# A two-layer GLA and differential-attention trunk: first root from token-major x, turned attention weights in pieces of 512 bytes, another stored order

## The chip, the cores and the metric

The kernel runs on one core of a Trainium2 chip. The metric is the device time of one execution in microseconds (us). A core has engines that run side by side: TensorE (PE; its weight loads are listed apart as PEld), VectorE (DVE), ScalarE (ACT), GpSimd (POOL), and SyncE (SP), which in this kernel issues every transfer (DMA). Each engine works through its own queue in order, so an instruction that waits holds up all that stand behind it.

## The reference, cut to what matters

x is 2048 tokens by 1024 features, in float32. Two layers; each computes

```python
h = rms_norm(x, norm_g[l]) * (1.0 + scale[:, None]) + shift[:, None]   # scale, shift from c
proj = h @ w_in[l]                                     # 1024 -> 3600 columns, split in nine
gqkv = silu(causal_depthwise_conv(gq, gk, gv))         # 4 taps
o_gla  = gla_branch(...)    # 4 heads: per chunk of 64 tokens state = a * state + k_dec^T v, o = q state
# diff_branch, 4 heads with two 64-wide maps each, block-causal in chunks of 64:
s = einsum('bqhmd,bkhmd->bhmqk', qi, k);  p = softmax(where(mask, s, -inf))
attn = p[:, :, 0] - lam * p[:, :, 1]
o = einsum('bhqk,bkhe->bqhe', attn, v)                 # then rms_norm, gate
x = x + gate[:, None] * (concat([o_gla, o_diff]) @ w_out[l])
```

`rms_norm` needs, for each token, the root of the mean of its 1024 squares. The last product of the attention, o = attn v (PV), sums over keys. TensorE sums over the partitions of its stationary operand, so the weights must lie with the keys on the partitions, while the softmax leaves them with the queries there: each 128x128 tile of weights has to be turned.

## The kernel before, in words

**Tiling.** The 2048 tokens are four units u of 512 (UT); a unit is four tiles of 128 (TT, P). Activations are feature-major (features on partitions, eight blocks k of 128; KT). The projections and the output projection work in split precision: a float32 operand is split in a rounded high part and a low rest (`hi`, `lo`), and three matmuls of 128x128 by 512 columns replace one. The score matmuls use two, the PV matmuls plain float32; TensorE shows each PV matmul as two records.

**Streams.** Python generators write the work of one kind each: `dense_stream` (projections of 9 weight items and the output), `gla_stream`, `qk_stream`, `attn_stream`, `prep_stream` (the normalized h of the next unit), `ada_stream` (modulation). `run_streams` interleaves them by a rough clock: `yield pe(cost, wait)` lets time pass, `yield need(event, lag)` holds a generator until another calls `done(event)`. Nothing is issued yet: `Program.record` notes each operation with what it depends on.

**Order.** `Program.order` is a list scheduler. It prices each operation (`cost`), gives tile buffers in the order in which they were recorded, adds prices such as a change of matmul `mode`, and picks on each engine, among what is ready, the operation with the smallest turn. The turns are the recorded order plus a stored list of steps, `ORDER` (a compressed text at the end of the file), which `found_order` unpacks. The engines get their instructions in the resulting order, for good: line 351 of the profile is where all of them are issued, so instructions are told apart by tiles.

**Start** (`start`, line 658). The vectors, c, and the first unit's x (feature-major, four transfers of 512 KB to tiles `xp`) are loaded. The squares of the eight feature blocks are made on ACT and summed on DVE into `sqs` (`add_square`); `sum_squares` sums over partitions with float32 matmuls against ones; `root` scales on DVE (`xms`) and takes the power on GpSimd (`rs`); four scaled identities and matmuls with ones spread the root to all partitions (`rsb`). Then, for each k, two DVE passes over a modulation weight tile `wm` give scale and shift, `make_h` makes `hhi` and `hlo`, and 24 matmuls of the first two projection items (0 and 4) follow, with weights `raw` split on ACT and DVE to `w`.

**Preparation of the later units** (`prep_gen`, line 634). In layer 0 a unit's x is loaded token-major (`xt`, four transfers of 512 KB), ACT squares it with an accumulated sum per token (`xss`), `rs_write` makes the root, transposes it and writes it to DRAM (`rd`); it is read back spread over partitions (`rsb`). This begins when the h of the unit before is done, plus 6 us of the rough clock. `make_h` waits for the event `free_h`. Tiles `xt`, `xp`, `la`, `E`, `qh`, `ql` share four buffers.

**GLA** (`gla_gen`, line 785). The gates pass through `la`, cumulative sums by matmuls with `trir`, and `E`, their exponential on ACT; transposes of the convolved keys and values (`uT`) follow, the values' ending with the event `vtr`; then the scan with 64x64 float32 matmuls (`Sn`, `vN`).

**Attention** (`attn_gen`, line 1005). For each head and query tile qt both score maps are made, reduced to a minimum by DVE, exponentiated on ACT into tiles `s` of up to 2048 keys, and combined on DVE into `at`. The weights of the unit's own keys are transposed on TensorE (`flip`). Those of earlier units' keys are *turned* (`turn_blocks`, line 1061) in units 1 and 2, and in unit 3 for heads 0 to 2: DVE transposes 32x32 blocks into `b`, a transfer writes `b` to a DRAM buffer `ad`, another reads it back to `at` with the blocks exchanged between partition groups. Two key blocks are interleaved element by element, so the read moves runs of 2 x 32 = 64 words (256 bytes), and `pv` (line 1072) loads each key block as stationary operand with a step of two words. V is stored in a matching order of rows (`vp`).

Of the kernel before, what the change touches and what calls it, by code (L numbers as in the profile page):

```python
# [13 lines left out]
F32 = mybir.dt.float32  # L14
# [110 lines left out]
class Program:  # L125
# [54 lines left out]
    def cost(e, method, args, kw, out):  # L180
        n = math.prod(out.shape[1:])
        if e == "S":
            return math.prod(out.shape) * 4 / {64: 208.0, 256: 326.0}.get(out.shape[-1], 350.0)
# [23 lines left out]
    def mode(op):  # L207
# [4 lines left out]
        return 1 if (k, m) == (CH, CH) else 2 if m == 32 else 0  # L212

# [13 lines left out]
    def order(self, turn_of):  # L227
# [27 lines left out]
        res, burst, mode = [], 0, 0  # L255
        while len(res) < N:
# [98 lines left out]
def trunk_kernel(ctx, tc, xl, x, c, ccol, w_ada, w_mod, w_all, w_glr, w_gk, vecs, lam, out):  # L355
# [278 lines left out]
    def prep_gen(l, u, xsrc):  # L634
        key = l * NU + u
        if l == 0:
            yield need("h", key - 1, lag=6.0)
            ss = p_sm.tile([P, TT], F32, tag="xss", name="xss", bufs=2)
            for t in range(TT):
# [3 lines left out]
                yield pe(0, 2.0)  # L643
            rs_write(key, ss)
# [13 lines left out]
    def start():  # L658
# [6 lines left out]
        sqs = p_x.tile([P, UT], F32, tag="sqs", name="sqs")  # L665
# [6 lines left out]
        for c_ in range(KT // 2):  # L672
# [9 lines left out]
        V.tensor_scalar(cact, cact, 0.5, None, op0=ALU.mult)  # L682
        wm = [mod_load(0)]
# [17 lines left out]
        for k in range(KT):  # L701
            if k % 2 and k + 1 < KT:
                for it in FIRST:
# [234 lines left out]
    AD = [[dram.tile([2 * u, P, 4, 64], F32, name=f"ad{u}_{t}") for t in range(2 * TT)] if u else None  # L938
# [66 lines left out]
    def attn_gen(l, u, hd):  # L1005
# [55 lines left out]
        def turn_blocks(at, b, dr):  # L1061

            n = u * UT
            src = at[:, 0:n].rearrange("p (g k a i) -> p g k a i", k=2, a=4, i=32)
            dst = b[:, 0:n].rearrange("p (g a i k) -> p g k a i", a=4, k=2, i=32)
            for k in range(2):
                V.transpose(dst[:, :, k], src[:, :, k])
            SY.dma_start(dr.rearrange("g p b n -> p g (b n)"), b[:, 0:n].rearrange("p (g n) -> p g n", n=256))
            SY.dma_start(at[:, 0:n].rearrange("p (h n) -> p h n", n=64),
                         dr.rearrange("g (a j) b n -> (j b) (g a) n", a=4))  # L1070

        def pv(qt):
# [19 lines left out]
            if turned:  # L1092
                pairs = at[:, 0:u * UT].rearrange("p (g m k) -> p g k m", k=2, m=P)
# [4 lines left out]
                for j in range(u):  # L1098
                    mmv(4 * j, 4, lambda k: pairs[:, k // 2, k % 2, :], False, j == u - 1)
# [218 lines left out]
def _layouts(x, c, w_ada, b_ada, norm_g, w_in, conv_w, w_gk, b_gk, gla_norm_g, qn_g, kn_g, lam_q1, lam_k1, lam_q2,  # L1318
# [25 lines left out]
    '{Wp48S^xk9=GL@E0stWa8~^|S5YJf5;FqgLq+I|2U>bnck+!@@V3AjytBp45^Tr3;$E~Z9ORR0R@5I(P6(V1^7&ZjV2!e;h2L-hkd023f?~QmHvy'  # L1344
    'fVakgbngi`>5pSg!9l?VM7NkTVkBM~8!=J<NRDIXxkw7gR>+Mzu#6ox-7gALO}P(vg^BQ|*#<DX6#e_Ss5mBRgq7-fGY*lsojHoNzyEiIa4UJWz8'
    'c#AtO|+deNLnfv>aknmGZ#JNvnX-Uu_G1P2cy%qJ4uh9B~8%EzPjvuT+HL=dBv@@?D3fG(Nrf>XNCz=^(mtyf7LUVR%@S#A9a+WvCZ(Toy!b+jDJ'
    'id$_S$)6>jQ$z@m)6UfabaK`+Oi>BaMz^;fF%?VT(0DlHe9sqDm_55`_o)!lXg*2Z`^vB0sZ!$Z2mAw*$z8sRQhT-<u~{nb%%n(I9{=A?7IQXo`}'
    'oX%VtS2;IPT<_e79BjY^~Fe*l9P(-HoSN~M23h|0<p!3`aHg#=PAe@IYNree>oF0Fc)zH|6K7~!>KWGLxeIviTYeaiyZ7@*HeIXf&AME8t5wxXiP'
    '0T{Ig0K@0N*k$uhgE88;;ZL;F(h%{_l3{1lM5MGgGxf@yRhGQs*mKFG8%KERO}?x02?Z9%`#AeB{IFM}p0pnTQa$TQR>9udIO;=-_5{Lt(4C!R+@'
    'ByJ#10S4YQwmkvbRkDf}YOq0(*mMPK^%(28Y0@7^Y-`<J{JDv*a)-N8FmaQ%ndNT(4YPH6#lSokDgAjKzr53NKjLJN>k^o&c-zdWCb`05~oX`uwh'  # L1350
    '|8A%aNL?0^YrziZ7C4uXwt8H1-FWuX$!ruQ6OvwxbA}q)lJ*_Lt4lR#P+JU913#>`6;lYN9EgX`Bnh8kLmL#mfd;naoRP0JV<5GF2-yPgwpOf>H6'
    'r9%$6pRjJ_nUv_BRl#|V~VO7Tg>QVb<#u5eex<ea+vla2edqnbd03__qM`GZ2gPm6_yh~U)P)1l@ppX?dqs8Zy8`QH0h>}D4CG5`ClE=z|9~_cIy'
    'BnRV%P`M!F)|`h^<I6$mPt{WvoGwyNb0@>090HwJGKf{U`J)YbJk!`Ls6qz~3#^W8fr+-kM+Q70Wlv!MpTY9fS3d8c51b}40IutrQpYN{(d19R%l'
    '0j2WIIs64$!pK-L>h5j=jXpmQCygS><q}PTHfy_jwi+6mEIxxZj)kNx{7-uE*5Q<lOsWeH(S7{j_b{b~qVEkl#G`u$3;~Vy1qsN~H)6TuRW5eif*'
    'SX%a}fh4>xwDJt1{cTQqu$snK-r#c2*R6J~Xr2xgEem!eS8t)M0EjFUgNcR*C~MOnmuhs$!;Fldg78;Q1cc0~<KazD}<^g5yK&tVlEck3Xvp-aIU'
    '0O@n8`3GbyzQSdDV{4_CH4*reN;eB>aY4o;nZ<D(!v4N)iktF13C~q3Y_7v>M2_&Q8Uo>>HZy-KCVsMSG*UgDwk&UU1S5(|ppP0C?Cw(|Ae1G*Mr'
    '0tQJbhqq{n<-VocAx3=!CI<qk=HCN%K!{}Aq)3R_z06^H}>)i`bM%hC3h}wljZshV%g2vX}Q%&`BaX^CqPK6UHZ~vxD|w{?2NYt_arRB5W%Z9Tq)'
    'r+bTe0rLFQNEr?IdGA7wm;6${Ajg1UX-{7$9Sy5)`Bsp?gND*5hWx9PXyKh8ypIJQ!AJe-KdeTuE~FNQTB!TdlIjY4X*J;DXB#3nL8g_F}r8L5g0'
    'laaoRJJarB$7Dj%I1xO02E>2a+M}WzCjK#8>yTqm1q0jHEF|DJq_wVAH&?8A+L;@pfT5jt!b2#hN}aK0$=}{vWWXDozC+*u2wP!An7idnS{sy0pC'
    '7lJHbscX$?M{YKzUF^I%9^T4=H|^g!sP;bI2_-B&mYl=Se`2sm?wef{Gu&)&^`@^%lrThhCixq+43I8ES3zOT~KF9UurJzjOWwGDR0+k4zZ)CVjk'  # L1360
# [208 lines left out]
```

## Time and profile before

| | |
|---|---|
| median of 3 runs | 2433.13 us (2430.43 to 2433.43) |
| the profiled execution | 2430.82 us, span 2428.7 us |
| TensorE with work in flight | 2372.0 us (98% of the span) |
| VectorE / ScalarE / GpSimd busy | 1829.6 / 1230.7 / 125.6 us |
| transfers | 573.77 MB, 369,525 packets, mean 236 GB/s |

The span runs from the first to the last instruction on the core. A matmul's busy time is modelled, and matmuls overlap: the distance from start to start of two neighbours tells what one takes. A group's row reads: line, engine, operation, out<-in by the program's names, shape, count | busy us, mean ns of one | idle time of the engine just before them, and what ended it. In the order of time a row gives its start, its length, and in brackets how long the engine stood idle before it and for what.

### The profile page before, as it was taken

The page shows a single profiled execution, that of the slowest core. Times are in us where ns is not written, and L with a number is a line of the kernel's source. Part 1 is how long each engine was busy: PE and PEld are TensorE (multiplying, and loading weights), DVE is VectorE, ACT ScalarE, POOL GpSimd, SP SyncE. Part 2 cuts the span into 40 slices and gives each one's busy share as a digit, 9 for nine tenths or more (in the row PEclk, how much of TensorE's full clock was granted, in tenths as well). Part 3 has the DMA queues.
Part 4 walks back from the last instruction along what each step waited for, and adds up shares of the span by engine and source line. Part 5 has one row for each costly group of instructions (what it writes and reads, how often), then busy time and mean ns, then how long its engine had stood idle before and what let it go on. Part 6 is the DMA issues. An engine that isn't in the chain of part 4 may idle for free.

```text
span 2428.7 us, 38475 instructions
## 1 busy us (share of the span) xinstructions
PE 2372.0 (98%) x12903; PEld 1945.9 (80%) x12903; DVE 1829.6 (75%) x5166; ACT 1230.7 (51%) x2726; POOL 125.6 (5%) x400
## 2 busy tenths in 40 slices
PE   6899999999999999999999999999999999999999
PEld 5687787888888888888788787888788887888887
DVE  8868886897568967589865894668746798747894
ACT  3766653556335553355663574346524556324552
POOL 0000000000000000000000000000000000000000
PEclk9899999999999999999999999999999999999999
DMA  7657997787776778587557777666667867775764
GB/s 293 241 193 259 324 338 245 251 270 239 246 230 204 248 223 276 171 247 236 181 198 270 270 276 263 215 222 216 211 244 231 244 205 235 232 257 172 232 193 150
DMA packets 369525, 573.77 MB, mean 236 GB/s; under 512 B 191824, under 2 KB 251696, under 8 KB 366256
## 3 DMA queue, kind: packets, MB, share of 16 engines
q1 hardware_dynamic: 369328, 571.32, 71.6%
q8 instruction: 102, 1.67, 0.3%
q14 instruction: 95, 0.78, 0.1%
HBM read 416.03 MB, written 161.50 MB: 238 GB/s over the span
## 4 chain that ended last, share of the span: by engine, by line
PE 78%; DVE 11%; ACT 4%; DMA 4%; issue 2%; POOL 0%; SPq 0%; DVEq 0%; ACTq 0%; POOLq 0%
PE acc L351 52%; PE sc L351 12%; PE po L351 9%; PE tp L351 5%; DVE s L351 4%; DMA w<-wd 2%; ACT s L351 1%; DVE w L351 1%; DVE t L351 1%; DVE xp L351 1%; ACT la L351 1%; DMA xp<-xd 1%; DVE vN L351 1%; DVE hlo L351 1%; DMA wr<-in_w_ada_dram 1%
## 5 line engine op out<-in xcount | busy, mean ns | idle before, releaser
L351 PE MATMUL acc<-w,hhi 128*128 128x512 f32 x2560 | 844.8, 405 | 7.0 <-DVE t L351 2.9
L351 PEld LDWEIGHTS acc<-w,hhi 128*128 128x128 f32 x2560 | 467.1, 189 | 102.3 <-DVE t L351 4.1
L351 PE MATMUL acc<-w,hlo 128*128 128x512 f32 x1280 | 496.5, 402 | 0.3 <-DVE hlo L351 0.3
L351 ACT ACTIVATE s<-s,mx 128x1280 f32<-128x1280 f32 (+15 forms) x256 | 308.3, 1205 | 317.0 <-DVE s L351 201.5
L351 DVE TENSOR_SCALAR_CACHE_REDUCE s<-sc,mx 64x64 f32<-64x64 f32 (+5 forms) x640 | 307.1, 483 | 61.8 <-PE sc L351 44.1
L351 PE MATMUL acc<-oh,w 128*128 128x512 f32 x1024 | 335.9, 398 | 2.0 <-DMA w<-wd 1.6
L351 PE MATMUL acc<-hhi,w 128*128 128x512 f32 x960 | 323.3, 401 | 0.6 <-DVE z L351 0.4
L351 PEld LDWEIGHTS acc<-w,hlo 128*128 128x128 f32 x1280 | 240.6, 189 | 45.8 <-issue 0.9
L351 PEld LDWEIGHTS po<-Vj,s 128*128 128x128 f32 x1536 | 215.6, 196 | 13.7 <-issue 0.6
L351 PEld LDWEIGHTS acc<-oh,w 128*128 128x128 f32 x1024 | 190.5, 188 | 44.2 <-DMA w<-wd 2.7
L351 PE MATMUL po<-Vj,s 128*128 128x128 f32 x1536 | 221.8, 280 | 0.0
L351 DVE TENSOR_SCALAR_CACHE_REDUCE s<-sc 128x512 f32<-128x512 f32 (+4 forms) x256 | 157.9, 620 | 80.9 <-PE sc L351 44.7
L351 PEld LDWEIGHTS acc<-hhi,w 128*128 128x128 f32 x960 | 178.0, 188 | 37.3 <-DVE z L351 1.1
L351 DVE SCALAR_TENSOR_TENSOR s<-s,r 128x512 f32<-128x512 f32 (+3 forms) x320 | 201.2, 666 | 3.6
L351 PE MATMUL acc<-ol,w 128*128 128x512 f32 x512 | 199.7, 397 | 0.0
L351 PE MATMUL acc<-hlo,w 128*128 128x512 f32 x480 | 189.3, 399 | 0.0
L351 PE MATMUL sc<-Kj,qh 128*128 128x512 f32 x384 | 157.6, 416 | 1.6 <-DVE s L351 0.9
L351 PE MATMUL sc<-Kj,ql 128*128 128x512 f32 x384 | 150.7, 398 | 0.0
L351 POOL MEMSET s<- 64x64 f32 x256 | 37.3, 146 | 2084.6 <-PE po L351 1150.7
L351 DVE SCALAR_TENSOR_TENSOR t<-ub,vec,t 128x512 f32<-128x512 f32 x192 | 138.8, 745 | 7.1 <-ACT t L351 6.4
L351 ACT CAST w<-raw 128x512 fp32r<-128x512 f32 x160 | 97.2, 622 | 79.0 <-PE acc L351 58.2
L351 DVE TENSOR_TENSOR w<-raw,w 128x512 fp32r<-128x512 f32 x160 | 108.1, 685 | 33.5 <-ACT w L351 32.8
(185 smaller groups left out, 3643.5 us busy)
## 6 DMA issues: line engine op xcount, KB each, us to landing
w<-wd SPq DMA_DIRECT2D x416, 512.0 KB, 4.5
wd<-w SPq DMA_DIRECT2D x144, 512.0 KB, 5.1
raw<-in_w_all_dram SPq DMA_DIRECT2D x80, 512.0 KB, 4.7
Kj<-kd SPq DMA_DIRECT2D x48, 512.0 KB, 6.1
ad<-s SPq DMA_DIRECT2D x24, 768.0 KB, 5.2
s<-ad SPq DMA_DIRECT2D x24, 768.0 KB, 6.9
wr<-in_w_ada_dram SPq DMA_DIRECT2D x128, 128.0 KB, 3.7
ad<-s SPq DMA_DIRECT2D x32, 512.0 KB, 4.0
```

The source lines that it names most:

```text
L351: getattr(self.engines[e], method)(*[real(a) for a in args], **{k: real(v) for k, v in kw.items()})
```

## The change

1. *Start.* The root of the first unit comes from token-major x, as in the later units: four transfers of 512 KB to tiles `xt` (in the ring of `s`), four Squares on ACT with accumulated sums, and `root` of these. The feature-major x, still wanted by `make_h`, is loaded one pair of blocks at a time, the first before the first modulation weights, the others in the loop over k. The eight squares, seven adds and the sums by matmul go.
2. *Preparation.* In layer 0 it begins at the event `vtr` of the unit before in place of `h` plus 6, and the rough clock lets 8 us pass between the squares and the root.
3. *Turned weights.* Four key blocks are interleaved instead of two: four DVE transposes per tile, each a quarter of the row, writing with a step of four words; `ad` is half as many groups with 128-word rows; the transfer out has runs of 512 words, the one back runs of 128 words (512 bytes); `pv` loads the stationary operand with a step of four words.
4. *Planner and order.* The price of a transfer by run length gets an entry for 128; a 64x64 matmul is priced at 70 ns instead of 54; a change to a `short` operation (a transpose, or a plain float32 matmul) costs 32 ns. `ORDER` is another stored list.

```diff
-                return 54 if args[1].shape[0] == CH else 60
+                return 70 if args[1].shape[0] == CH else 60
...
+                if self.short(ops[i]) != brief:
+                    brief = not brief
+                    t += 32 if brief else 0
...
-            yield need("h", key - 1, lag=6.0)
+            yield need("vtr", key - 1)
...
                 yield pe(0, 2.0)
+            yield pe(0, 8.0)
             rs_write(key, ss)
...
-        sqs = p_x.tile([P, UT], F32, tag="sqs", name="sqs")
+        ss = p_sm.tile([P, TT], F32, tag="xss", name="xss", bufs=2)
+        xt = []
+        for t in range(TT):
+            if t % 2 == 0:
+                xt.append(p_s.tile([P, 2, D], F32, tag="s", name="xt"))
+            SY.dma_start(xt[-1][:, t % 2, :], x[t * P:t * P + P, :])
...
+        x_load(0)
         wm = [mod_load(0)]
...
-        for k in range(KT):
-            add_square(sqs, xs[k // 2][:, k % 2, :], k == 0)
-        root(sum_squares(sqs))
+        for t in range(TT):
+            A.activation(xt[t // 2][:, t % 2, :], xt[t // 2][:, t % 2, :], AF.Square, accum_out=ss[:, t:t + 1])
+        root(ss)
...
             if k % 2 and k + 1 < KT:
+                x_load((k + 1) // 2)
...
-    AD = [[dram.tile([2 * u, P, 4, 64], F32, name=f"ad{u}_{t}") for t in range(2 * TT)] if u else None
+    AD = [[dram.tile([u, P, 4, 128], F32, name=f"ad{u}_{t}") for t in range(2 * TT)] if u else None
...
-            src = at[:, 0:n].rearrange("p (g k a i) -> p g k a i", k=2, a=4, i=32)
-            dst = b[:, 0:n].rearrange("p (g a i k) -> p g k a i", a=4, k=2, i=32)
-            for k in range(2):
+            src = at[:, 0:n].rearrange("p (g k a i) -> p g k a i", k=4, a=4, i=32)
+            dst = b[:, 0:n].rearrange("p (g a i k) -> p g k a i", a=4, k=4, i=32)
+            for k in range(4):
                 V.transpose(dst[:, :, k], src[:, :, k])
-            SY.dma_start(dr.rearrange("g p b n -> p g (b n)"), b[:, 0:n].rearrange("p (g n) -> p g n", n=256))
-            SY.dma_start(at[:, 0:n].rearrange("p (h n) -> p h n", n=64),
+            SY.dma_start(dr.rearrange("g p b n -> p g (b n)"), b[:, 0:n].rearrange("p (g n) -> p g n", n=UT))
+            SY.dma_start(at[:, 0:n].rearrange("p (h n) -> p h n", n=P),
                          dr.rearrange("g (a j) b n -> (j b) (g a) n", a=4))
...
-                pairs = at[:, 0:u * UT].rearrange("p (g m k) -> p g k m", k=2, m=P)
+                pairs = at[:, 0:u * UT].rearrange("p (g m k) -> p g k m", k=4, m=P)
...
-                    mmv(4 * j, 4, lambda k: pairs[:, k // 2, k % 2, :], False, j == u - 1)
+                    mmv(4 * j, 4, lambda k: pairs[:, k // 4, k % 4, :], False, j == u - 1)
```

More of the change, by code (lines that the diff above doesn't have):

```diff
@@ L182, in cost @@
         if e == "S":
-            return math.prod(out.shape) * 4 / {64: 208.0, 256: 326.0}.get(out.shape[-1], 350.0)
+            return math.prod(out.shape) * 4 / {64: 208.0, 128: 277.0, 256: 326.0}.get(out.shape[-1], 350.0)
         if e == "T":
@@ L212, in mode, with short @@
         return 1 if (k, m) == (CH, CH) else 2 if m == 32 else 0
+    @staticmethod
+    def short(op):
+        return op[1] == "transpose" or op[2][2].dt == F32
     @staticmethod
@@ L254, in order @@
         work, win = {}, 3413
-        res, burst, mode = [], 0, 0
+        res, burst, mode, brief = [], 0, 0, True
         while len(res) < N:
@@ L670, in mod_load, with x_load @@
             return wm
-        for c_ in range(KT // 2):
+        def x_load(c_):
             xp = p_q.tile([P, 2, UT], F32, tag="q", name="xp")
@@ L1343 @@
 ORDER = (
[L1344 to L1358, printed above, removed]
@@ new lines @@
+    'OnuYWqg5GaamQH5fW#>e-^KB9gyIphC-t+Aigfi?VUBm|IFVMf|GX2hqjNL;y+Yyw8*gF3V813_Jm7(I>vQ4OTyl@!Qjnk_>@IqP9b>Xz<M0wIMk'
+    'FL502k##i1FSE*mOcHOLd9hey2Cl~z%D~L=CTuJOXm~OdpOCx@b{gkcFd^(!V{NZ-Cob3Lm|;AB;TrKXAX3JmKAtDIQS6>@icA#33D!<iJbl?g=J'
+    'O>?NHhRY;1on5%Kpi?74zu8-4isa+5n@to*$*<dF9q1mlI}eBN|Pc9-E7zP|qDB*v#PnIu4*y?e-BdEckOc3PFC@4xJ*gqi|YCVEP1fKOHP>e<pn'
+    'Kta!|Oq;EhBriDZ)EpO+faaAmuja@?hQ@$o6R*AzqGy>?;?`HX+6L0b_j#@0!#QO*e1DZ&FWn`V4B<p_-6!`D&JlYm|MK^1=R~YXQTHN+$i#bAmF'
+    'YkQ90=z}YQ&;=^ZEcR63?xj2mcDH1L2pWy{xZy?xijg;;Lj(jBh2=obf2DVKrwPlXrMAKg5^6pFjArg6~Wxu~2Ccppi+P3QSecP}~4`X-N_rG2ek'
@@ L1547 @@
+    'l{DK(D<hT2NJ03vMk<AroSsH>%^|p5`mOPF7EY~%E(6CUCXYJHy945pa6(!Q+ALB+UCc$y3@`M7A9t)c*5fWyzz{p!}8B1RBtQy&80I8GZ<~QO{i'
+    'b2X&#3NWrj~k4iNwBv0Q~*%(u|xT+>}Q@q2UJLuyqqqgg18j>1aw%q?!=r|7koawyOha+qDudf)*s$hG=zsHVb)fduVA=!lt*(Quz9?&^MS*W>rv'
+    'jTQQf&$j7Kr07?$#yjJEItP};2WWF`{HkV$U%gx#1x8suQ~DjFu0zW_lw+ViSf&pI}u$_cIj%qnfpS+12#ZMAk@n)rQ5q5uE@b$-I?hP&IR00FOv'
+    '0rs&1XBw=qvBYQl0ssI200dcD'
 )
```

375 lines of the change are left out of this document (187 added, 188 removed).

## The prediction

> **What bounds the kernel now.** I read the page first: busy times, then the chain of work that ended last.
>
> ```profile
> span 2428.7 us, 38475 instructions
> PE 2372.0 (98%) x12903; PEld 1945.9 (80%) x12903; DVE 1829.6 (75%) x5166; ACT 1230.7 (51%) x2726; POOL 125.6 (5%) x400
> ...
> PE 78%; DVE 11%; ACT 4%; DMA 4%; issue 2%; POOL 0%; SPq 0%; DVEq 0%; ACTq 0%; POOLq 0%
> ```
>
> TensorE has work in flight for 2372.0 of 2428.7 us. So only two things move the time: what its own instructions take, and the 56.7 us in which it stands idle. The profiled execution took 2430.8 us, 2.1 us more than its span; the median of the three runs shown is 2433.1, another 2.3 us (0.1%) above. I sum against 2430.8.
>
> Next, the view of who waited for whom, for TensorE alone, and the table of busy times by stretches of 50 us (columns: PE, PEld, DVE, ACT, POOL, granted clock, DMA share, GB/s).
>
> ```profile
> PE sc L351 <- DVE sqs L351: 17.0, 1, 17.0
> PE tp L351 <- ACT E L351: 9.7, 2, 9.3
> PE tp L351 <- DVE s L351: 4.7, 6, 2.1
> PE acc L351 <- DMA w<-wd: 2.3, 6, 0.7
> ...
> 0.00:50.00 50.00, 27.63 (x109) 22.98 (x110) 39.29 (x104) 18.18 (x29) 2.40 (x11) 1.00 0.88 340
> 100.00:150.00 50.00, 38.06 (x179) 30.82 (x179) 31.99 (x118) 29.24 (x91) 4.55 (x15) 0.83 0.50 176
> ...
> 1200.00:1250.00 50.00, 49.64 (x285) 41.54 (x286) 35.46 (x118) 35.01 (x82) 3.48 (x13) 0.91 0.40 144
> ...
> 2000.00:2050.00 50.00, 49.61 (x260) 39.06 (x260) 48.33 (x126) 24.79 (x50) 3.07 (x10) 1.00 0.79 253
> ```
>
> The idle time sits in two places: the start (22 of the first 50 us) and the stretch from 100 to 150 us, with 12 us idle and the clock at 0.83. Elsewhere TensorE is full; the rest of its waits are single ones of 0.3 to 2 us. No wait of TensorE for the turned weights' transfers is listed.
>
> **The start.** Today the root is made from feature-major x: eight squares, seven adds on DVE, eight matmul records.
>
> ```profile
> 3.13 7.17 DMA xp<-in_xl_dram
> ...
> 11.50 5.47 DVE L351 TENSOR_TENSOR sqs<-t,sqs 128x512 f32<-128x512 f32 x7 [2.55 <-ACT sqs L351]
> ...
> 17.02 1.87 PE L351 MATMUL sc<-ones,sqs 128*128 128x1 f32 x8 [17.02 <-DVE sqs L351]
> ...
> 20.38 0.15 DVE L351 TENSOR_SCALAR xms<-sc 128x4 f32<-128x4 f32 x1
> ...
> 26.31 0.80 PE L351 MATMUL acc<-w,hhi 128*128 128x512 f32 x1 [2.22 <-ACT hhi L351]
> ```
>
> The x tiles land at 10.30 (3.13 + 7.17), the scaling of the sum starts at 20.38, and from there to the first projection matmul it is 5.93 us. The change puts four token-major x transfers (the same 2 MB) where the four feature-major ones were, and four Squares with an accumulated sum in place of adds and matmuls. One such Square is 1.054 us plus 0.187 for the readout:
>
> ```profile
> L351 ACT ACTIVATE xt<-xt 128x1024 f32<-128x1024 f32 x12 | 12.6, 1054 | 7.0 <-DMA xt<-in_x_dram 7.0
> L351 ACT ACTIVATION_READ_ACCUMULATOR xt<-xt 128x1 f32 x12 | 2.2, 187 | 0.0
> ```
>
> If three are done when the last tile lands, the sums are ready at 10.3 + 1.24 = 11.5; if all four land together, at 10.3 + 4 x 1.24 = 15.3. With 5.93 and 0.2 us behind, the first matmul comes at 17.6 to 21.4, that is 4.9 to 8.7 us sooner; I take **-7**. Against it: x is now fetched twice, 2 MB or 6 us at the 340 GB/s of the first stretch, whose engines are 0.88 busy, and the first modulation weights are issued one transfer (0.6 us) later. After 26.31 TensorE ran without a wait to 104 us, so what it gains here it keeps, unless those 6 us come back (rival below).
>
> **Unit 1's preparation.** At 104.9 TensorE stops for 9.26 us.
>
> ```profile
> 106.89 0.33 SPq L351 DMA_DIRECT2D xt<-in_x_dram  x1
> ...
> 112.22 1.06 ACT L351 ACTIVATE xt<-xt 128x1024 f32<-128x1024 f32 x1 [4.07 <-DMA xt<-in_x_dram]
> 113.19 0.19 ACT L351 ACTIVATION_READ_ACCUMULATOR xt<-xt 128x1 f32 x1
> 113.40 1.08 ACT L351 ACTIVATE E<-sc 128x512 f32<-128x512 f32 x2
> ...
> 114.14 0.45 PE L351 MATMUL tp<-ident,s 128*128 128x128 f32 x1 [9.26 <-ACT E L351]
> ```
>
> ScalarE's queue stands behind a Square of the next unit's x, whose transfer was issued at 106.89. The exponentials E queued behind it free the PSUM tiles that TensorE wants. ACT was free at 108.15 (112.22 - 4.07); E began at 113.40. The change moves these transfers and Squares behind the GLA value transposes of the previous unit, so 5.25 us of the 9.26 go. The remaining 4.0 us, the 2.1 us wait at 122.9 and the slow clock may stay: 0.17 x 50 = 8.5 us of clock were lost in this stretch, about half of it under work. Bounds 0 (another wait takes over) and -16 (9.3 + 2.1 + half of 8.5); I take **-8**, the 5.25 and a part of the clock.
> The Trainium skill (TensorE: Matmul & The Clock Gate, "What's actually happening") says the clock halves after an idle window of about 3.4 us; the row of 0.83 agrees. By it 4.0 us left idle would still halve the clock, the gain here would be 5, and the time 3 us longer.
>
> **The turned weights on TensorE.** The weight loads of the PV matmuls now step over 4 words instead of 2 (16 bytes instead of 8). 88 tiles are turned; 672 matmuls, two records each, read them: 1344 of the 1536 records below. The last head's are not turned.
>
> ```profile
> L351 PEld LDWEIGHTS po<-Vj,s 128*128 128x128 f32 x1536 | 215.6, 196 | 13.7 <-issue 0.6
> L351 PEld LDWEIGHTS po<-Vt,s 128*128 128x128 f32 x640 | 96.2, 194 | 15.0 <-ACT s L351 2.6 <-POOL s L351 1.3 <-issue 0.9
> ...
> 1114.33 2.99 PE L351 MATMUL po<-Vj,s 128*128 128x128 f32 x24
> ...
> 2395.82 1.06 PE L351 MATMUL po<-Vt,s 128*128 128x128 f32 x8
> ...
> 408.71 0.58 PE L351 MATMUL sc<-ones,am 128*128 128x1 f32 x4 [1.10 <-DVE am L351]
> ```
>
> With 0.28 us for the last record of a run, step 2 issues one every (2.99 - 0.28)/23 = 118 ns, contiguous weights one every (1.06 - 0.28)/7 = 111 ns. So step 2 already costs 6 to 7 ns. Four records that move a single column take 0.58 us together, about 0.11 us each, no less than those that move 128: in this type the load, not the moving side, may set the pace. Step 4 has no row. Bounds: nothing more, or another doubling of the load, 111 ns x 1344 = 149 us. I take half of the known step, 3 ns: **+4**, since that row is nearest, and keep +13 ns (17 us) for the range.
>
> **The transposes on DVE.** Two per tile become four, 176 more, each half as long.
>
> ```profile
> L351 DVE STREAM_TRANSPOSE s<-s 128x768 f32<-128x768 f32 x48 | 45.7, 966 | 0.2
> L351 DVE STREAM_TRANSPOSE s<-s 128x512 f32<-128x512 f32 x64 | 44.2, 701 | 0.3
> L351 DVE STREAM_TRANSPOSE s<-s 128x256 f32<-128x256 f32 x64 | 27.2, 435 | 0.3
> ```
>
> 265 ns for 256 elements more, so 170 ns are fixed: 176 x 0.17 = 30 us on DVE at most. It is 75% busy, so most hides; in stretches like 2000 to 2050 (48.33 of 50 us) it does not, and uncovered it would all be paid. I take **+1**, bounds 0 and +10. Should writing at step 4 double the 1.04 ns an element, 86,016 elements add 89 us of DVE; that goes with the rival on steps.
>
> **The transfers.** Reading back, 64-word pieces become 128-word ones.
>
> ```profile
> DMA packets 369525, 573.77 MB, mean 236 GB/s; under 512 B 191824, under 2 KB 251696, under 8 KB 366256
> ...
> ad<-s SPq DMA_DIRECT2D x24, 768.0 KB, 5.2
> s<-ad SPq DMA_DIRECT2D x24, 768.0 KB, 6.9
> ```
>
> The same bytes take 6.9 us back against 5.2 us out in longer pieces: 1.7 us sooner at best. attn_gen plans 9 us of other work before the PV of a turned tile (WAIT), so this lies beside TensorE: **0**, bounds 0 and -2 (the 2.3 us of waits for w).
>
> **The order and its prices.** The planner's price for a pair of 64x64 records goes from 54 to 70 ns.
>
> ```profile
> L351 PE MATMUL po<-Sn,qT 64*64 64x128 f32 x512 | 22.0, 277 | 0.0
> L351 PE MATMUL sc<-vN,E 64*64 64x128 f32 x512 | 21.6, 277 | 0.0
> ```
>
> 22.0 us for 256 pairs is 86 ns, so the new price is nearer, and a plan made with it should meet fewer waits than the dozen of 0.3 to 2 us. But it also reshuffles everything: **-3**, bounds -12 and +12.
>
> **Sum**: -7 - 8 + 4 + 1 + 0 - 3 = -13, so 2430.8 - 13 = 2417.8, **2418**. The forecast's own range, with the middle bounds, is 2402 to 2428.
>
> **Rivals.**
>
> *Unit 1 comes late.* The wait removed at 104.9 returns at the boundary of units 0 and 1.
>
> ```profile
> 213.26 0.60 PE L351 MATMUL tp<-ident,uT 128*128 128x128 f32 x4
> ...
> 230.03 1.33 ACT L351 ACTIVATE hhi<-xp,B 128x512 fp32r<-128x512 f32 x2
> ...
> xt<-in_x_dram SPq DMA_DIRECT2D x12, 512.0 KB, 5.3
> rsb<-rd SPq DMA_DIRECT2D x7, 256.0 KB, 3.6
> ```
>
> The value transposes end at 213.86 and h of unit 1 begins at 230.03: 16.2 us. Behind the transposes now come transfer 5.3, Square 1.24, root and transpose about 2, the write of the root about 1.5, its broadcast 3.6, scaling about 1.5: 15.1 us, if SP's queue lets the four transfers go at once. Behind weight transfers of 4.5 us each it is late by 5 to 10 us, with a slow clock behind it: about 13 us, all of the gain: **2431**. Against it: the new order may put the value transposes earlier. Units 2 and 3 have more room.
>
> *Step 4 is slow (the other side).* Place: every turned weight load, and DVE's writes. It decides from 13 us / 1344 = 10 ns a record on: at 128 ns a record the gain is gone, at twice the load (118 + 111) the kernel takes 2418 - 4 + 149 = **2563**. For it: step 2 already costs 6 to 7 ns, and the load seems to be what paces these records. Against it: DVE's transposes, written at step 2, take 1.04 ns an element with no sign of a step, and 6 ns is small. The Trainium skill (SBUF — State Buffer, "Specifications (TRN2)") says that two hits on a 16-byte line are needed for full bandwidth: step 2 would be free, step 4 not. The trace agrees only in part, since step 2 isn't free, and no row here shows step 4. By that rule the time is up to this rival's 2563.
>
> *The start gives its gain back.* The second copy of x, 2 MB at 340 GB/s, delays the weights of the first projections by 6 us; TensorE starts early and waits at the second or third k: 2418 + 6 = **2424**.
>
> **How the numbers follow.** Forecast 0.50; start given back 0.08; unit 1 late or other waits of the new order 0.22, around 2431 and spread to both sides (0.04 faster, 0.12 same, 0.06 slower); step 4 costing over 10 ns 0.16. Half of the rest, 0.02 each, for faster by more than the forecast's range and for the same. A difference under 0.2% (4.9 us) can't be told from none. Faster: 0.50 + 0.08 + 0.04 + 0.02 = 0.64, of which I move 0.03 to the same since the forecast's upper end lies at the bound: 0.61. Same: 0.12 + 0.02 + 0.03 = 0.17. Slower: 0.06 + 0.16 = 0.22. Range: 2398 (start -8.7, preparation -16, order -8) to 2446 (only 5 us gained at the start, step 4 at +17, DVE +1, and the 2.3 us by which the median lies above); the doubled load lies outside.
>
> **What would show it.** Start: first projection matmul between 17.6 and 21.4 us instead of 26.31. Preparation: no E behind a Square near 105 us, and the stretch 100 to 150 with a clock above 0.83. Step: runs of PV records at 118 to 124 ns; 128 or more overturns the sign. DVE: 352 transposes at 300 to 570 ns; twice that shows slow writes. Late unit: a TensorE wait of over 3 us for hhi before unit 1's first projection. The page: packets under 512 bytes fall by about 86,000. I am wrong if TensorE's busy time rises by more than its idle time falls.

## The result and the profile after

| | before | after |
|---|---|---|
| median of the runs, us | 2433.28 (2430.43 to 2436.53) | 2558.62 (2557.95 to 2559.26) |
| ratio, 95% interval | | 1.0521 (1.0507 to 1.0534) |
| span of the profiled execution, us | 2428.7 | 2557.5 |
| TensorE busy / not busy, us | 2372.0 / 56.7 | 2508.6 / 48.9 |

The change makes the kernel 125 us slower. The likeliest forecast, 2418 us, and its range up to 2446 were wrong. What came is the rival *Step 4 is slow*, priced at 2563 us.

The page of the changed kernel, its busy times, groups and packets:

```profile
span 2557.5 us, 38700 instructions
...
PE 2508.6 (98%) x12895; PEld 2089.5 (82%) x12895; DVE 1882.8 (74%) x5335; ACT 1234.5 (48%) x2726; POOL 122.7 (5%) x400
...
DMA packets 262582, 575.87 MB, mean 225 GB/s; under 512 B 19856, under 2 KB 122736, under 8 KB 259312
...
L358 PEld LDWEIGHTS po<-Vj,s 128*128 128x128 f32 x1536 | 350.8, 309 | 6.8 <-issue 1.1
L358 PE MATMUL po<-Vj,s 128*128 128x128 f32 x1536 | 355.5, 375 | 0.1
```

And the matmul row of the same group before; the prediction shows its load row:

```profile
L351 PE MATMUL po<-Vj,s 128*128 128x128 f32 x1536 | 221.8, 280 | 0.0
```

TensorE is not starved: its idle time fell by 8 us while its busy time rose by 137. By far the largest rise is in the PV matmuls of the turned weights: their loads grew from 215.6 to 350.8 us, 196 to 309 ns each, and the matmul records from 221.8 to 355.5 us.

The changed kernel's records in order of time (start, length, operation, count) show what one such record takes, in a run of twelve like the run of 24 that the prediction read:

```profile
1085.73 2.96 PE L358 MATMUL po<-Vj,s 128*128 128x128 f32 x12
```

With 0.4 us for the last record, (2.96 - 0.4)/11 = 233 ns from start to start. Before it was 118 ns.

The same kernel's groups on DVE, shapes kept apart:

```profile
L358 DVE STREAM_TRANSPOSE s<-s 128x384 f32<-128x384 f32 x96 | 80.3, 863 | 0.3
L358 DVE STREAM_TRANSPOSE s<-s 128x256 f32<-128x256 f32 x128 | 77.0, 629 | 0.7
L358 DVE STREAM_TRANSPOSE s<-s 128x128 f32<-128x128 f32 x128 | 46.5, 396 | 0.3
```

(863 - 396)/256 = 1.82 ns an element, where it was 1.04: these writes step over four words too. The group takes 204 us of DVE where it took 117.

The start, in order of time (in brackets how long the engine was idle and for what), and the stretch of 100 to 150 us (columns as in the prediction):

```profile
17.51 2.07 PE L358 MATMUL tp<-t,ones 128*128 128x128 f32 x8 [17.51 <-DVE t L358]
21.80 1.22 PE L358 MATMUL acc<-w,hhi 128*128 128x512 f32 x2 [2.21 <-ACT hhi L358]
```

```profile
100.00:150.00 50.00, 46.55 (x221) 37.45 (x222) 38.67 (x142) 33.37 (x110) 6.44 (x23) 0.90 0.58 205
```

The first projection matmul comes at 21.80 instead of 26.31, and TensorE is busy for 46.55 of these 50 us instead of 38.06. So TensorE gains time at both places, as the forecast hoped, and the gain is buried under what the step costs.

### The profile page after: what moved, and what is told of

The parts are those of the page before. It is cut to its first block, busy times and chain, and to the rows that moved or that the text cites. A ratio compares the mean times of both kernels' runs of the same rounds, so it can differ in the third digit from the quotient of the medians.

```text
span 2557.5 us, 38700 instructions
## 1 busy us (share of the span) xinstructions
PE 2508.6 (98%) x12895; PEld 2089.5 (82%) x12895; DVE 1882.8 (74%) x5335; ACT 1234.5 (48%) x2726; POOL 122.7 (5%) x400
## 5 line engine op out<-in xcount | busy, mean ns | idle before, releaser
L358 PE MATMUL acc<-w,hhi 128*128 128x512 f32 x2560 | 835.9, 401 | 5.0 <-ACT hhi L358 2.2
L358 ACT ACTIVATE s<-s,mx 128x512 f32<-128x512 f32 (+15 forms) x256 | 308.0, 1203 | 310.9 <-DVE s L358 185.3
L358 PEld LDWEIGHTS po<-Vj,s 128*128 128x128 f32 x1536 | 350.8, 309 | 6.8 <-issue 1.1
L358 PE MATMUL po<-Vj,s 128*128 128x128 f32 x1536 | 355.5, 375 | 0.1
L358 PE MATMUL acc<-hhi,w 128*128 128x512 f32 x960 | 315.7, 398 | 3.3 <-issue 1.6
L358 DVE STREAM_TRANSPOSE s<-s 128x256 f32<-128x256 f32 (+2 forms) x352 | 203.8, 608 | 1.3
L358 ACT ACTIVATE junk<-po 128x128 f32<-128x128 f32 x128 | 35.6, 278 | 255.9 <-PE po L358 255.6
```

The costliest lines, as they stand in the source:

```text
L358: getattr(self.engines[e], method)(*[real(a) for a in args], **{k: real(v) for k, v in kw.items()})
```

## The experiments

All kernels below have the order of their instructions written out, so that an edit doesn't reshuffle the rest. Ratios are to the kernel before, run beside them on the same chip.

### Loads and writes of step 4, each alone

Three versions of the changed kernel take the step out of the loads (e1), out of the writes (e5), and out of both (e6). Transfers, shapes and counts stay.

```diff
 e1, e6: the stationary operand is 128 words side by side
-  pairs = at[:, 0:u * UT].rearrange("p (g m k) -> p g k m", k=4, m=P)
+  pairs = at[:, 0:u * UT].rearrange("p (g k m) -> p g k m", k=4, m=P)
 e5, e6: the transposes write side by side
-  dst = b[:, 0:n].rearrange("p (g a i k) -> p g k a i", a=4, k=4, i=32)
+  dst = b[:, 0:n].rearrange("p (g k a i) -> p g k a i", a=4, k=4, i=32)
```

> The changed kernel, every engine's instructions in the same order; PV loads its turned weights as 128 words next to each other instead of with a step of 4 (so the words of a key block are the wrong ones; transposes and transfers are as in the changed kernel). Theory 'loads' (the step of the weight load alone makes the kernel slower): records of the turned PV come every 111 ns instead of 232, 1344 x 121 ns = 163 us less, 2396 us. Rival 'writes' (DVE's transposes, at 1.8 ns an element instead of 1.04, and the wider interleave make the weights late): nothing changes on that side, 2550 to 2560 us. Rival 'order' (the new order is worse): 2550 to 2560 us.

> The changed kernel, same order; the four transposes of a tile write their words next to each other instead of with a step of 4 (the key blocks arrive wrongly sorted), PV still loads with a step of 4. Theory 'loads': DVE's transposes fall back to 1.04 ns an element, some 68 us less DVE work, and the time stays within 5 us of 2558. Rival 'writes': most of the 154 us come back, 2410 to 2450 us.

> The changed kernel, same order and same transfers of 512-byte runs; neither the transposes write nor the loads read with a step (the blocks are wrongly sorted). Theory 'two costs' (loads some 130 us, slow writes the rest, hidden while TensorE is slow): against the flat loads alone (2445 us) the writes give back 30 to 36 us, 2409 to 2415 us, level with two blocks at step 2 (2417) or up to 8 us below it. Rival 'order' (the 2445 us come from the new order): within 5 us of 2445.

| us (ratio, interval) | writes at step 4 | writes side by side |
|---|---|---|
| loads at step 4 | after: 2558.62 (1.0521) | e5: 2545.72 (1.0468, 1.0452 to 1.0484) |
| loads side by side | e1: 2444.69 (1.0055, 1.0041 to 1.0069) | e6: 2413.49 (0.9931, 0.9916 to 0.9946) |

The loads cost 132 us with quick writes (2545.72 - 2413.49) and 114 with slow ones. The writes cost 31 us while TensorE is quick (2444.69 - 2413.49) and 13 when the loads slow it. Together they are 145 us, and without both (e6) the changed kernel is 0.7% faster than before, some 17 us by the ratio. "Loads" was right on the cause and wrong that nothing else matters: e1 was expected at 2396, and e5 within 5 us of 2558. "Two costs" held: e6 was expected at 2409 to 2415.

The timeline of e1 shows the loads back at the pace of contiguous ones, (2.84 - 0.28)/23 = 111 ns:

```profile
1064.10 2.84 PE L356 MATMUL po<-Vj,s 128*128 128x128 f32 x24
```

Who waited for whom on TensorE, first in e1, then in e6:

```profile
PE sc L356 <- DVE s L356: 7.2, 18, 1.0
PE tp L356 <- DVE s L356: 6.5, 13, 1.2
```

```profile
PE tp L356 <- DVE s L356: 4.6, 10, 1.0
PE sc L356 <- DVE s L356: 2.4, 5, 0.9
```

The slow writes come out as many short waits for DVE's softmax tiles s, of about a microsecond at most. These rows hold 7 of the 31 us more. Where the rest lies was not placed stop by stop.

### The turning alone, in the old kernel

e3 is the kernel before, start and order too, with only part 3 of the change: the interleaving by four (transposes, `AD`, the two transfers, the loads). e12 is e3 with its loads side by side, so that of the step only the writes are left.

```diff
 e3, e12
-            src = at[:, 0:n].rearrange("p (g k a i) -> p g k a i", k=2, a=4, i=32)
-            dst = b[:, 0:n].rearrange("p (g a i k) -> p g k a i", a=4, k=2, i=32)
-            for k in range(2):
+            src = at[:, 0:n].rearrange("p (g k a i) -> p g k a i", k=4, a=4, i=32)
+            dst = b[:, 0:n].rearrange("p (g a i k) -> p g k a i", a=4, k=4, i=32)
+            for k in range(4):
...
 e12
-                pairs = at[:, 0:u * UT].rearrange("p (g m k) -> p g k m", k=2, m=P)
+                pairs = at[:, 0:u * UT].rearrange("p (g k m) -> p g k m", k=4, m=P)
```

> The kernel before, with its order, its start and its preparation; only the turning is changed to four key blocks, step 4 and runs of 512 bytes (the two added transposes stand right behind the two there are). Theory 'loads': 2433 + 153 = 2586 us, a few us more where DVE is full. Rival 'order': within 10 us of 2433, since the old order is kept.

> The kernel before, old order, old start: four transposes per tile that write with a step of 4, runs of 512 bytes, but contiguous weight loads (the words of a key block are the wrong ones). Against it stands the same pair of edits in the changed kernel's order (2445 us; with contiguous writes 2413). Theory 'slow writes cost wherever TensorE is quick': the loads give 7 us, the 50 us more of DVE work take 20 to 30, 2445 to 2455 us. Rival 'only the new order is too tight for them': 2424 to 2430 us.

e3: 2560.86 us, ratio 1.053 (1.0516 to 1.0545): the whole loss and 2 us more, with nothing of the start, the preparation or the new order. It issues TensorE's records in the same sequence as before, so I summed the distances from start to start by the kind of record that begins them. The span grew by 130.7 us. Intervals that begin at a PV record grew by 134, all others together shrank by 3: 1269 that run on to another such record grew from 147.4 to 255.7 us, 150 that run on to a projection by 16, and the 117 to all else by 9. The timeline of e3:

```profile
1099.69 5.30 PE L349 MATMUL po<-Vj,s 128*128 128x128 f32 x22
```

(5.30 - 0.4)/21 = 233 ns. Not every record pays: where a PV record stands behind a projection matmul of 512 columns, the distance is 232 ns before and 234 in e3, medians of 141. Its load begins with that matmul and runs while the columns pass. That is why 1165 of these intervals grew, by 115 ns in the median, and not as many as the 1344 turned records, and why the time came out 25 us under the 2586 expected.

e12: 2461.61 us, ratio 1.0119 (1.0106 to 1.0133). Slow writes alone cost the old kernel 29 us by the ratio, more than expected, and some 37 if the 6 to 7 ns are counted that its loads gained by lying side by side. The waits of e12; before had 2.6 us in the first row, 9.7 in the second and 4.7 in the third:

```profile
PE sc L349 <- DVE s L349: 11.3, 23, 1.1
PE tp L349 <- ACT E L349: 9.8, 2, 9.3
PE tp L349 <- DVE s L349: 6.7, 9, 2.1
```

### What sets the price of a step

If reading costs by the 16-byte line, step 3 should cost three quarters of step 4, and steps above 4 no more than 4. e4 is the changed kernel with another step for each unit's loads, e13 the one with contiguous loads (e1) and another step for each unit's writes.

```diff
 e4
+  step = ((3, 8, 12), (1, 6, 5))[l][u - 1]
...
+  return at[:, c0:c0 + step * P].rearrange("p (m k) -> p k m", k=step)[:, k % 4 % step, :]
 e13
+  step = ((3, 8, 2), (1, 6, 5))[l][u - 1]
+  V.transpose(b[:, 0:n // 4 * step].rearrange("p (m k) -> p k m", k=step)[:, k % step, :]
+              .rearrange("p (g a i) -> p g a i", a=4, i=32), src[:, :, k])
```

> The changed kernel, same order; PV's weight loads take another step in each unit: in layer 0 step 3 in unit 1, 8 in unit 2, 12 in unit 3; in layer 1 step 1 in unit 1, 6 in unit 2, 5 in unit 3 (the words are those of other keys; only the pace is of interest). Theory 'one word to a 16-byte line': a load pays as soon as neighbouring words lie 16 bytes or more apart, and no more beyond: 111 ns a record at step 1, 232 at 5, 6, 8 and 12; at step 3, where one pair of words in three shares a line, between 118 and 232. Rival 'distance' (the cost grows with the step, 57 ns for each word beyond 2): 175 at step 3, 290 at 5, 346 at 6, 460 at 8, 690 at 12.

> The changed kernel's order with contiguous weight loads; the transposes write with another step in each unit: in layer 0 step 3 in unit 1, 8 in unit 2, 2 in unit 3; in layer 1 step 1 in unit 1, 6 in unit 2, 5 in unit 3 (the weights end up in wrong places). From the loads (111 ns a record at step 1, 117 at 2, 174 at 3, 232 at 4 for 32, 64, 96 and 128 lines of 16 bytes) the theory 'lines' has 1.81 ns for each line that an access pattern touches. It expects of the writes 1.04 ns an element at steps 1 and 2, 0.75 x 1.81 = 1.36 at step 3, and 1.8 at 5, 6 and 8. Rival 'any step over 2 doubles': 1.8 at step 3 too; rival 'distance': over 2 at 5, 6 and 8.

e4 took 2547.74 us, e13 2451.06 (one run each; only the pace within the run is used). Runs of PV records in e4, one for each unit, in the order of steps 3, 8, 12, 1, 6 and 5:

```profile
425.99 1.49 PE L356 MATMUL po<-Vj,s 128*128 128x128 f32 x8
...
752.65 3.97 PE L356 MATMUL po<-Vj,s 128*128 128x128 f32 x16
...
1086.11 3.37 PE L356 MATMUL po<-Vj,s 128*128 128x128 f32 x12
...
1610.39 1.05 PE L356 MATMUL po<-Vj,s 128*128 128x128 f32 x8
...
1876.22 3.62 PE L356 MATMUL po<-Vj,s 128*128 128x128 f32 x16
...
2216.17 5.39 PE L356 MATMUL po<-Vj,s 128*128 128x128 f32 x24
```

DVE's transposes in e13 by stretch, in the order of steps 3, 8, 2, 1, 6 and 5 (count, busy us, mean ns):

```profile
L356 DVE STREAM_TRANSPOSE s<-s 128x128 f32<-128x128 f32 x64 | 20.0, 337 | 0.2
...
L356 DVE STREAM_TRANSPOSE s<-s 128x256 f32<-128x256 f32 x56 | 35.6, 668 | 1.3 <-PE po L356 0.5 <-issue 0.4
...
L356 DVE STREAM_TRANSPOSE s<-s 128x384 f32<-128x384 f32 x48 | 26.8, 569 | 0.1
...
L356 DVE STREAM_TRANSPOSE s<-s 128x128 f32<-128x128 f32 x64 | 19.6, 306 | 0.5
...
L356 DVE STREAM_TRANSPOSE s<-s 128x256 f32<-128x256 f32 x48 | 30.5, 648 | 3.3 <-PE po L356 2.2 <-ACT s L356 0.7
...
L356 DVE STREAM_TRANSPOSE s<-s 128x384 f32<-128x384 f32 x32 | 28.1, 900 | 2.3 <-PE po L356 1.6 <-ACT s L356 0.6
```

Loads: distances between records, medians over the unit, good to about 1 ns (the first distance of a run behind a 512-column matmul is shorter, 108 ns in the first row shown). Writes: the mean less 165 ns that are fixed, by the number of elements; step 4 is from the kernel after.

| step in words | 1 | 2 | 3 | 4 | 5 | 6 | 8 | 12 |
|---|---|---|---|---|---|---|---|---|
| 16-byte lines that 128 words touch | 32 | 64 | 96 | 128 | 128 | 128 | 128 | 128 |
| load, ns a record | 111 | 117 | 174 | 232 | 222 | 222 | 238 | 267 |
| write, ns an element | 1.10 | 1.05 | 1.34 | 1.82 | 1.91 | 1.89 | 1.96 | |

232/128 = 1.81 ns a line. 96 lines then make 174 ns, as measured, and 64 lines make 116, also as measured; 32 lines would make 58, but 111 ns is a floor that something else sets. The writes follow the same price, 0.75 line x 1.82 = 1.37 ns an element at step 3, above a floor of about 1.05. So within these two runs the rule is: the larger of the floor and 1.8 ns for each 16-byte line touched. It holds to 5% for the loads up to step 8 (222 to 238 ns against 232) and to 8% for the writes. The 267 ns of step 12 aren't explained by it; that stays open.

### The version with two blocks, and how long the pieces must be

e2 is the changed kernel (its start, preparation, planner and order) with two blocks as before: step 2, pieces of 256 bytes. e11 has no interleaving at all: one transpose per tile, contiguous loads, pieces of 128 bytes.

```diff
 e2, against after
-            for k in range(4):
+            for k in range(2):
...
-            SY.dma_start(at[:, 0:n].rearrange("p (h n) -> p h n", n=P),
+            SY.dma_start(at[:, 0:n].rearrange("p (h n) -> p h n", n=64),
...
-                pairs = at[:, 0:u * UT].rearrange("p (g m k) -> p g k m", k=4, m=P)
+                pairs = at[:, 0:u * UT].rearrange("p (g m k) -> p g k m", k=2, m=P)
 e11, against e2
-            for k in range(2):
-                V.transpose(dst[:, :, k], src[:, :, k])
+            V.transpose(b[:, 0:n], at[:, 0:n])
...
-            SY.dma_start(at[:, 0:n].rearrange("p (h n) -> p h n", n=64),
+            SY.dma_start(at[:, 0:n].rearrange("p (h n) -> p h n", n=32),
...
-                pairs = at[:, 0:u * UT].rearrange("p (g m k) -> p g k m", k=2, m=P)
+                pairs = at[:, 0:u * UT].rearrange("p (k m) -> p k m", m=P)
```

> The changed kernel with its start, its preparation and its order (every engine's sequence kept, two of the four transposes of each tile left out), but two key blocks interleaved as in the kernel before: step 2, runs of 256 bytes. Theory 'loads': 1344 x (232 - 118) = 153 us less than the changed kernel, 2405 us, so the rest of the change gains 25 to 30 us on the kernel before. Rival 'order': no faster than the kernel before, 2433 us or more. Rival 'pieces' (the 512-byte runs bring part of that gain): 2410 to 2425 us, with waits for the transfers back.

> The changed kernel's start, preparation and order with no interleave at all: one transpose per tile, contiguous weight loads, runs of 128 bytes back from DRAM. Theory 'runs are hidden': against two blocks (2417 us) the loads give 6.5 ns on some 1130 records, 7 us, and DVE has some 14 us less to do: 2405 to 2412 us, the fastest of all. Rival 'runs matter': the transfers back come late and TensorE waits for them: over 2417 us.

e2: 2417.43 us, ratio 0.9941 (0.9929 to 0.9954). It beats both kernels: the rest of the change is worth 14 us by the ratio, and the four blocks lose 141 (2558.62 - 2417.43). That is 12 us short of the gain that theory "loads" expected; the time lies in the range of rival "pieces", but the waits for the transfers back that belong to it do not show. e2 and the kernel after issue TensorE's records in the same sequence, so they can be compared as before and e3 were: intervals that begin at a PV record are 144 us longer in the kernel after, 1250 of them by 115 ns in the median, and the others together 1 us shorter. The new order thus hides fewer of the slow loads than the old one did in e3 (1165). e11: 2450.5, ratio 1.008 (1.0065 to 1.0094), 33 us behind e2 and not ahead of it as expected. The waits of e11:

```profile
PE acc L356 <- DMA w<-wd: 9.6, 7, 3.7
PE po L356 <- DMA s<-ad: 6.8, 9, 1.8
```

e11 moves 585,140 packets instead of 370,101, and TensorE waits for projection weights and turned tiles. These rows hold 16 of the 33 us; the first does not appear in e2, and the second has 0.6 us there. The largest turned tiles land in 7.3 us instead of 6.3; the rest of the loss was not placed. So longer pieces do pay, from 128 to 256 bytes; from 256 to 512 nothing of that kind was left to gain (those 0.6 us).

### Where the 14 us of the start, the preparation and the order arise

To compare kernels with different orders, I priced every TensorE record at the median distance of its kind before, and read when each kernel had done the same amount of work. This is an estimate, good to a few us. By it e2 is ahead by some 4 us up to the work that the old kernel has done at 104 us, by 14 to 15 at 136 us, by 15 at 581 and again by 14 near the end; between them the lead falls to 8 or less. The windows of e2 agree (before: 77.29 us busy up to 100 us; then 38.06 at clock 0.83):

```profile
0.00:100.00 100.00, 80.71 (x354) 63.17 (x355) 84.47 (x231) 57.01 (x113) 2.94 (x15) 1.00 0.77 291
...
100.00:150.00 50.00, 45.54 (x237) 36.21 (x237) 39.41 (x142) 34.32 (x111) 6.61 (x23) 1.00 0.58 209
```

Is it the parts of the change, or the order they were planned into? Three versions of the kernel before, in its own order with two blocks, take one part each: e7 the new start; e8 the fourth Square of unit 1 (in a buffer of its own) behind the two exponentials E; e14 the third and fourth transfer and Square, the root and its write and read back, all at about 170 to 200 us.

```diff
 e7: start() as in the change, issued where the old start's operations stood
-        for k in range(KT):
-            add_square(sqs, xs[k // 2][:, k % 2, :], k == 0)
-        root(sum_squares(sqs))
+        for t in range(TT):
+            A.activation(xt[t // 2][:, t % 2, :], xt[t // 2][:, t % 2, :], AF.Square, accum_out=ss[:, t:t + 1])
+        root(ss)
 e8: the fourth Square two places later on ACT (e14: t >= 2, both in one osb tile, some 70 us later)
+                if u == 1 and t == 3:
+                    xt = p_o.tile([P, 4, UT], F32, tag="osb", name="xt").rearrange("p a n -> p (a n)")[:, 0:D]
+                else:
+                    xt = p_q.tile([P, D], F32, tag="q", name="xt")
```

> The kernel before with the changed kernel's start alone: token-major x and Squares at the places of the old transfers and squares, the other x pairs behind the second, fourth and sixth modulation weights; everything else in the old order. Theory 'kept': TensorE begins its projections 4 to 5 us sooner, as in the changed kernel (21.8 us instead of 26.3), and the end comes 4 to 5 us sooner, about 2426 us. Rival 'given back': it begins sooner and waits for weights or x behind the 2 MB more, 2430 to 2433 us.

> The kernel before with one instruction moved: the fourth Square of unit 1's x, at 112 us, stands behind the two exponentials E in ACT's queue instead of ahead of them; its tile lies in a buffer that is free there, since E takes the old one. Theory 'Square': E starts some 5 us sooner, the 9.3 us wait shrinks to about 4, and the time falls by 5 to 10 us, 2422 to 2427 us. Rival 'next wait': another wait ends TensorE's stop at the same time, 2430 to 2434 us.

> The kernel before, with its own order written out, in which only the preparation of unit 1 is moved: the transfers and Squares of its third and fourth x tile (in a buffer of the output tile instead of the ring of q), the root, its write and its read back go out at about 170 to 200 us instead of 101 to 119 us. Everything is computed. In the version with two blocks that kept the new start, the new preparation and the new order, TensorE reached the same amount of its work 4 us sooner up to 100 us, and 14 us sooner at 136 us. Theory 'the whole preparation must leave the stretch': with both late Squares and their transfers gone from ScalarE's queue at 105 to 113 us the stop of 9.3 us falls to about 4, nothing else takes its place, the 2.1 us wait near 123 us and a part of the slow clock go with it: 7 to 10 us, 2424 us. Rival 'the gain belongs to the new order': something else in the old order's queues takes the place as it did when one Square alone was moved behind the exponentials (9.26 became 7.74 in three pieces): 2431 to 2433 us. Rival 'unit 1 comes late': TensorE waits for hhi before unit 1's first projection near 230 us and gives all of it back: a wait of over 3 us there.

None moves the time by the 4.9 us that can be told from none: e7 2429.88 (0.9993, 0.9984 to 1.0002), e8 2430.69 (0.9997, 0.9988 to 1.0006), e14 2430.5 (0.9991, 0.9982 to 0.9999).

In e7 the gain is lost within the start. Its timeline:

```profile
13.73 1.03 POOL L349 TENSOR_TENSOR rs<-xms,mhalf 128x4 f32<-128x4 f32 x1 [12.01 <-DVE xms L349]
16.79 1.23 DVE L349 SCALAR_TENSOR_TENSOR wm<-wm,cb 128x1024 f32<-128x1024 f32 x1 [3.15 <-DMA wm<-in_w_mod_dram]
...
20.56 0.87 DVE L349 TENSOR_SCALAR t<-ident,rs 128x128 f32<-128x128 f32 x4
...
25.71 0.79 PE L349 MATMUL acc<-w,hhi 128*128 128x512 f32 x1 [2.74 <-ACT hhi L349]
```

The root is there at 14.76 (13.73 + 1.03), but the scaled identities that spread it stand on DVE behind two passes over `wm`, whose transfer lands at 16.79, and a split of weights. The first projection matmul comes 0.6 us sooner, not 4.5. Theory 'kept' falls, but not quite for the rival's reason: most of the time is lost ahead of that matmul, on DVE and in its wait for `wm`, and not behind it.

TensorE's stops around 105 us in e8, then in e14:

```profile
109.32 0.45 PE L349 MATMUL tp<-ident,s 128*128 128x128 f32 x1 [3.89 <-ACT E L349]
113.58 0.77 PE L349 MATMUL po<-Vt,s 128*128 128x128 f32 x2 [3.18 <-ACT s L349]
```

```profile
107.72 0.45 PE L349 MATMUL tp<-ident,s 128*128 128x128 f32 x1 [2.85 <-ACT E L349]
112.68 0.66 PE L349 MATMUL sc<-Kt,qh 128*128 128x384 f32 x1 [2.87 <-DVE s L349]
121.11 0.90 PE L349 MATMUL tp<-ident,s 128*128 128x128 f32 x3 [2.10 <-DVE s L349]
```

In e8 the Square still holds up ScalarE, now ahead of a softmax tile. In e14 it is gone from there; yet the stop of 9.26 us returns as shorter ones along the chain of exponentials and softmax tiles, and the clock stays as slow as before. Two windows of e14:

```profile
110.00:120.00 10.00, 5.25 (x14) 3.31 (x14) 8.17 (x33) 4.49 (x17) 1.63 (x4) 0.50 0.38 153
...
100.00:150.00 50.00, 41.09 (x191) 32.37 (x190) 33.16 (x121) 29.30 (x94) 4.51 (x16) 0.83 0.42 156
```

Over the 50 us e14 is busy 3 us longer than before, and is 2 us ahead at their end. In the old order little other work stands ready for TensorE at this place. In e2, with the new order, there is more: 237 matmuls in these 50 us instead of 191 in e14, six waits of 0.4 to 1.0 us, and a granted clock of 1.00. Theory 'the whole preparation must leave the stretch' falls; 'the gain belongs to the new order' is what is left, by exclusion. No run puts the start and the preparation together into the old order, or the new order onto the old preparation, and which of the planner's new prices found that order was not tried.

## Why the prediction was wrong, step by step

- **The step that failed: the turned weights on TensorE.** "Step 4 has no row. ... I take half of the known step, 3 ns: +4, since that row is nearest". Measured: 232 ns instead of 118, 144 us against e2 in intervals that begin at a PV record. The mistake was to read the 6 to 7 ns of step 2 as a slope. They were the place where a second limit rises above the first: 64 lines x 1.81 = 116 against a floor of 111. From there on doubling the lines doubles the time. The prediction itself held the hint, "the load, not the moving side, may set the pace", and its upper bound of 149 us was close to the price; only the value between the bounds was chosen badly, and its chance of 0.16 was too low.
- **The rule cited against the change was nearer than the row.** The Trainium skill (SBUF — State Buffer, "Specifications (TRN2)") asks for two hits on each 16-byte line for full bandwidth. The runs agree for step 3 (174 ns), step 4 and above. For step 2 they refine it: it isn't free for these loads, because 64 lines already take 5 ns more than the floor.
- **The rival's price, 2563, was right to 4 us, partly by luck.** It put 111 ns on 1344 records, 149 us, and nothing more on DVE. Measured were 115 ns on some 1250 records, 144 us, as the others hide behind 512-column matmuls. The slow writes add 13 us (after against e5), but slower loads also take short waits away: from e6 to e5 the intervals that do not begin at a PV record shrink by 18 us. That these two nearly cancel was not foreseen.
- **The transposes on DVE: +1, bounds to +10.** "With no sign of a step" was true of step 2 only, since 0.5 line x 1.82 = 0.91 ns lies under the floor of 1.04. At step 4 the writes took 1.82 ns, three quarters more, near the doubling that the text named and gave to the rival. With the added transposes that is 87 us of DVE, 13 us of time here and 31 where TensorE is quick.
- **The start: -7.** Measured 4.5 us at the first projection matmul, at 21.80 just outside the 17.6 to 21.4, and 4 us kept in e2. Missing from the sum was DVE's queue between the root and the scaled identities: in the kernel after the root is there at 13.51, and the first identity starts at 17.17, behind two `wm` passes and a split of weights. The rival that the start gives its gain back through the second copy of x wasn't seen in e2, where the lead of some 4 us stands to 104 us.
- **The preparation: -8.** The place gained some 10 us in e2, so the size was near and the cause was not: taking the Squares out of the way gave 2 us in the trace (e14), and in the time no more than can't be told from none. The size was luck. The rival *Unit 1 comes late* did not come either: no wait for hhi of over 3 us is in the list of after.
- **Order and prices: -3, transfers: 0.** Beyond 136 us the new order's lead over before does not grow (14 to 15 there and near the end), so as far as that estimate goes the order's value lay in those 10 us. For the transfers, 0 was right from 256 to 512 bytes. e11 shows that the same term isn't 0 from 128 to 256.
- **The rest of the sum.** -7 - 8 + 0 - 3 = -18 without the two terms of the step; e2 gave -14 and e6 -17 by their ratios. The sum of these terms was near, partly because errors cancelled: 4 us instead of 7 at the start, some 10 instead of 8 + 3 at the stretch and the order, and for another cause than the text gave.
- **"I am wrong if TensorE's busy time rises by more than its idle time falls."** It rose by 136.6 and fell by 7.8. The sign was overturned, as announced, by records at 128 ns or more.
- **The count of packets.** Packets under 512 bytes fell by 172,000, not 86,000: every 256-byte piece leaves that class, and half as many 512-byte ones take their place outside it. Nothing in the sum hung on it.
- **The clock.** That "the row of 0.83 agrees" was too coarse a reading. The trace of before has the clock at half from 106.74 us, only 1.86 us after TensorE stopped at 104.88; the last section has more of this.

## What to carry to other kernels

A small surcharge at one size (117 against 111 ns) can be a second limit that has just overtaken the first: price the next size by the second limit's own law, floor against lines touched, before taking the surcharge as a slope. In float32, interleave for longer transfers only as far as every reader and writer in SBUF stays at two words or more on a 16-byte line: here 256-byte pieces at step 2 beat both 128-byte pieces at step 1 (by 33 us) and 512-byte pieces at step 4 (by 141 us). And a stop behind a named instruction need not go with it: take that instruction away in the same order first, and see what stands behind.

## What the runs showed of the hardware

- Loads of the stationary operand in float32 and DVE's transposed writes have the same price by the line, 1.81 and 1.82 ns for each 16 bytes touched, over floors of 111 ns a record and 1.05 ns an element. Step 12 cost more than step 4 (267 against 232 ns), which is unexplained.
- A slow load is hidden where the record ahead of it moves 512 columns: 232 ns before, 234 with step 4.
- The clock can halve without a long stop. In e14 it was at half from 107.06 us, 2.2 us into a stop that lasted 2.85, and stayed there for 17.07 us, with no idle stretch over 2.87 us. In the kernel after it was at half for 10.24 us, though no stop of TensorE there was longer than 1.01 us:

```profile
101.89:105.30 3.41, 1.53 (x7) 0.93 (x8) 3.28 (x13) 3.04 (x11) 0.64 (x2) 1.00 0.60 238
105.30:115.54 10.24, 9.15 (x34) 7.33 (x33) 8.82 (x38) 4.84 (x18) 1.66 (x6) 0.50 0.65 220
```

  The Trainium skill (TensorE: Matmul & The Clock Gate, "What's actually happening") speaks of an idle window of about 3.4 us; here TensorE was busy for 1.53 of the 3.41 us ahead of the drop. e2 has nearly the same stops at this place and kept a clock of 1.00, so stops of this size do not decide it alone; what does, no run here shows.
